# The down projection of one decoder layer as seven products of halves

## The chip, the core and the metric

One core of a Trainium2 chip runs the kernel once per call. Its engines work side by side: TensorE (PE: matmuls and their weight loads), VectorE (DVE), ScalarE (ACT), GpSimd (POOL), and SyncE (SP), which here only issues transfers. An engine does its instructions in the order of its program; waits between engines are semaphores. The metric is the device time of one call in microseconds (us), the lower the better.

## What is computed

One layer on 512 tokens of 1024 features, in fp32. Token mixing comes first and is not touched. The end of the layer is:

```
x  = x + merged @ w_out
up = conv(rms_norm(x) * ffn_norm @ w_up)        # 1024 -> 5632, causal, width 3
a  = silu(up[:2816]) * up[2816:]
x  = x + a @ w_down                              # 2816 -> 1024
out = x * rsqrt(mean(x * x) + 1e-6) * final_norm # over the 1024 features
```

## The kernel before

Every large fp32 product is done in three passes: each operand is split into a high part (a cast to the reduced format fp32r, on ACT) and a low part (the residue, a subtraction on DVE), and PE adds high x high, high x low and low x high (`split`, `wsplit`, `mm3`). Activations lie turned: features on the 128 partitions, the 512 tokens along the row, so that `hH[j]`, `hL[j]` are the parts of feature block j. Weights come through a pool `wp` with three buffers for each of three tags: `wr` (as loaded, 1024 columns, 512 KB, by `wtile` on SP's queue), `wh` and `wl` (the parts).

The up projection (`up`, `conv`) goes over 44 chunks of 128 features; each chunk is 24 matmuls of 128x512, then DVE, ACT, DVE, DVE scale and convolve it. Every second chunk gives one block of `a`, split into `aH[i]`, `aL[i]`, i = 0 to 21.

The down projection is done by feature: for output blocks j = 0 to 5 a bank `pd` sums 22 x 3 matmuls of 512 columns, weights as the stationary operand and `a` as the moving one. After each block DVE adds the residual `x1[j]`, ACT squares it, DVE sums the squares in `acc3`, ACT multiplies by the gain. For the last two blocks the weights `w_e` are loaded and split early (`eh`, `el`, in the memory that `hH`, `hL` leave); they are done for 384 tokens as above (`pA`, moving 384 columns) and for the last 128 tokens the other way round (`pB`, 256 columns), with tokens on the partitions. The norm of the 384 tokens is a mean over partitions (`rooted`, `over_partitions`) and is multiplied in while `pB` runs; that of the last 128 goes along the row, with six blocks turned by PE into `pTa`, `pTb`.

The order on each engine is set by a scheduler from the order and the dependences of the code: an instruction keeps to its engine's queue, and a tile of a pool waits until the tile that had its buffer is no longer read.

## Time and profile before

| | us |
|---|---|
| median of three runs (708.94 to 711.18) | 708.98 |
| the profiled execution | 709.26 |
| its span, from the first to the last instruction | 707.6 |
| PE busy in it | 699.6 |
| DVE busy | 476.5 |
| ACT busy | 331.5 |
| POOL busy | 12.3 |
| loads: 67 MB in all, mean over the span | 98 GB/s |

Times in the rows below count from the start of the span. The up projection's matmuls end at about 578.1, `pd` runs to 667.9, `pA` and `pB` to 701.2, and the output is written until 707.6. Busy time of PE is a sum of instructions that overlap one another (a 128x512 matmul is shown with 389 ns, while one starts each 0.23 us), so the pitch between starts is the measure, not the length shown.

### The profile page before, as it was taken

What the parts mean: (1) busy time and instruction counts of PE and PEld (TensorE: products, weight loads), DVE (VectorE), ACT (ScalarE), POOL (GpSimd) and SP (SyncE); (2) the same over time, 40 slices, a digit from 0 to 9 for tenths busy, and PEclk for the clock granted to TensorE, in tenths of its full rate; (3) what the DMA queues carried; (4) which work ended last, traced back from release to release, by engine and by line L of the source; (5) the groups of instructions that cost most, each with busy time, mean ns of one, the idle gap of its engine ahead of it and who ended that gap; (6) DMA issues with size and microseconds to landing.
All of it is one profiled execution on the core that took longest, in us unless ns stands there. A gap on an engine that the chain in (4) does not pass through costs nothing.

```text
span 707.6 us, 8629 instructions
## 1 busy us (share of the span) xinstructions
PE 699.6 (99%) x3303; PEld 586.6 (83%) x3303; DVE 476.5 (67%) x817; ACT 331.5 (47%) x496; POOL 12.3 (2%) x16
## 2 busy tenths in 40 slices
PE   9999999999999999999999999999999999999996
PEld 6888888888888888888888888888888888888896
DVE  8875799877777578755587777777677765433104
ACT  5464556676667533433454444444444444423101
POOL 0000110000000000000100000000000000000000
PEclk9999999999999999999999999999999999999999
DMA  8524422131121122523222233223322335631003
GB/s 260 179 77 135 168 83 82 60 113 40 69 72 60 33 87 76 190 94 105 93 98 89 90 102 107 90 90 100 108 89 91 95 98 163 194 87 48 0 1 120
DMA packets 22617, 69.63 MB, mean 98 GB/s; under 512 B 2736, under 2 KB 4400, under 8 KB 22576
## 3 DMA queue, kind: packets, MB, share of 16 engines
q1 hardware_dynamic: 21568, 66.72, 28.9%
q10 hardware_dynamic: 1008, 2.36, 0.9%
q8 instruction: 26, 0.43, 0.3%
q14 instruction: 15, 0.12, 0.1%
HBM read 66.97 MB, written 2.10 MB: 98 GB/s over the span
## 4 chain that ended last, share of the span: by engine, by line
PE 94%; DVE 3%; DMA 2%; issue 0%; ACT 0%; SPq 0%; POOLq 0%; DVEq 0%
PE pup L81 11%; PE pup L82 11%; PE pup L80 11%; PE pd L81 4%; PE pd L80 4%; PE pd L82 4%; PE pout L81 2%; PE pout L80 2%; PE pout L82 2%; PE pzb L82 2%; PE pzb L80 2%; PE pzb L81 2%; PE pv L80 2%; PE pv L82 2%; PE pza L81 2%; PE pv L81 2%
## 5 line engine op out<-in xcount | busy, mean ns | idle before, releaser
L70 ACT CAST wh_u<-wr_u 128x1024 fp32r<-128x1024 f32 x44 | 46.3, 1052 | 41.6 <-PE pup L81 29.5
L71 DVE TENSOR_TENSOR wl_u<-wr_u,wh_u 128x1024 fp32r<-128x1024 f32 x44 | 53.9, 1226 | 8.0 <-ACT wh_u L70 7.0
L604 DVE TENSOR_TENSOR z<-pup,r 128x512 f32<-128x512 f32 x44 | 30.2, 688 | 35.1 <-PE pup L82 35.1
L80 PE MATMUL pd<-aH,wh_d 128*128 128x512 f32 x132 | 51.3, 389 | 0.0
L81 PE MATMUL pd<-aL,wh_d 128*128 128x512 f32 x132 | 51.3, 389 | 0.0
L82 PE MATMUL pd<-aH,wl_d 128*128 128x512 f32 x132 | 51.3, 389 | 0.0
L70 ACT CAST wh_g<-wr_g 128x1024 fp32r<-128x1024 f32 x24 | 25.2, 1050 | 44.4 <-issue 23.3
L76 ACT CAST aH<-y 128x512 fp32r<-128x512 f32 x22 | 13.7, 621 | 56.7 <-DVE z L603 54.2
L71 DVE TENSOR_TENSOR wl_d<-wr_d,wh_d 128x896 fp32r<-128x896 f32 (+1 forms) x18 | 20.5, 1136 | 29.0 <-ACT wh_d L70 28.6
L70 ACT CAST wh_d<-wr_d 128x896 fp32r<-128x896 f32 (+1 forms) x18 | 17.7, 982 | 43.2 <-PE pd L81 35.2
L606 ACT ACTIVATE y<-z,part 128x512 f32<-128x512 f32 x44 | 35.9, 818 | 3.4 <-DVE z L604 1.8
L71 DVE TENSOR_TENSOR wl_g<-wr_g,wh_g 128x1024 fp32r<-128x1024 f32 x24 | 29.4, 1224 | 7.0 <-ACT wh_g L70 6.9
L610 DVE SCALAR_TENSOR_TENSOR y<-z,part,y 128x512 f32<-128x512 f32 x44 | 33.0, 752 | 1.4
L608 DVE SCALAR_TENSOR_TENSOR y<-z,part,y 128x512 f32<-128x512 f32 x44 | 32.8, 747 | 0.3 <-ACT y L606 0.3
L623 ACT ACTIVATE y<-y 128x512 f32<-128x512 f32 x22 | 13.9, 632 | 36.4 <-DVE y L610 36.4
L80 PEld LDWEIGHTS pd<-aH,wh_d 128*128 128x128 f32 x132 | 24.8, 188 | 5.2
L82 PEld LDWEIGHTS pd<-aH,wl_d 128*128 128x128 f32 x132 | 24.8, 188 | 5.2
L81 PEld LDWEIGHTS pd<-aL,wh_d 128*128 128x128 f32 x132 | 24.8, 188 | 5.1
L81 PE MATMUL pout<-mL,wh_o 128*128 128x512 f32 x64 | 25.4, 397 | 0.0
L82 PE MATMUL pout<-mH,wl_o 128*128 128x512 f32 x64 | 25.3, 395 | 0.0
L80 PE MATMUL pout<-mH,wh_o 128*128 128x512 f32 x64 | 25.2, 396 | 0.0
L77 DVE TENSOR_TENSOR aL<-y,aH 128x512 fp32r<-128x512 f32 x22 | 15.2, 693 | 14.2 <-ACT aH L76 14.2
(595 smaller groups left out, 2003.4 us busy)
## 6 DMA issues: line engine op xcount, KB each, us to landing
wr_u<-in_w_u_dram SPq DMA_DIRECT2D x44, 512.0 KB, 3.3
wr_g<-in_w_g_dram SPq DMA_DIRECT2D x24, 512.0 KB, 3.3
wr_d<-in_w_d_dram SPq DMA_DIRECT2D x12, 448.0 KB, 3.4
x<-in_xT_dram SPq DMA_DIRECT2D x16, 256.0 KB, 4.5
wr_v<-in_w_v_dram SPq DMA_DIRECT2D x8, 512.0 KB, 4.2
wr_o<-in_w_o_dram SPq DMA_DIRECT2D x8, 512.0 KB, 3.2
wr_d<-in_w_d_dram SPq DMA_DIRECT2D x6, 512.0 KB, 3.5
wr_e<-in_w_e_dram SPq DMA_DIRECT2D x5, 512.0 KB, 3.7
```

The lines of the kernel that those rows point to most:

```text
L70: A.copy(th[:, lo:hi], raw[:, lo:hi])
L71: V.tensor_tensor(out=tl[:, lo:hi], in0=raw[:, lo:hi], in1=th[:, lo:hi].bitcast(F32), op=ALU.subtract)
L76: A.copy(th, src)
L77: V.tensor_tensor(out=tl, in0=src, in1=th.bitcast(F32), op=ALU.subtract)
L80: T.matmul(o, lhsT=wh, rhs=xh, start=start, stop=False)
L81: T.matmul(o, lhsT=wh, rhs=xl, start=False, stop=False)
L82: T.matmul(o, lhsT=wl, rhs=xh, start=False, stop=stop)
L604: V.tensor_tensor(out=z[:, 2:], in0=pz, in1=r2, op=ALU.mult)
L606: A.activation(out=y, in_=z[:, 2:], func=AF.Identity, scale=part[:, w + 2:w + 3], bias=part[:, PCB + f:PCB + f + 1])
L608: V.scalar_tensor_tensor(out=y, in0=z[:, 1:S + 1], scalar=part[:, w + 1:w + 2], in1=y, op0=ALU.mult, op1=ALU.add)
L610: V.scalar_tensor_tensor(out=y, in0=z[:, 0:S], scalar=part[:, w:w + 1], in1=y, op0=ALU.mult, op1=ALU.add)
L623: A.activation(out=yg, in_=yg, func=AF.Silu)
```

## The change

The down projection becomes one product of two 2 x 2 matrices of halves: `a` by token halves (256 tokens) and by halves of its 2816 features (11 blocks), `w_down` by the same feature halves and by halves of the 1024 outputs. Eight products of halves become seven, after Winograd's form of Strassen's scheme:

- products of halves: P1 = A11 B11, P2 = A12 B21, P3 = S4 B22, P4 = A22 T4, P5 = S1 T1, P6 = S2 T2, P7 = S3 T3; in the code `product("1", ...)` to `product("7", ...)` in the order 1, 5, 2, 6, 3, 7, 4
- S1 = A21 + A22, S2 = S1 - A11, S3 = A11 - A21 on DVE, S4 = A12 - S2 on POOL; S2, S3 and S4 are written over A11, A21 and A12
- the differences of weights (`b11`, `b21`, `b22`, `t3_of`) are made on POOL, of weights as loaded, 1024 columns at a time (512 in the last step): T1 in product 1, T2 in product 2, T1 anew (B22 - B12) in product 3, and T4 = T2 - B21 in product 7
- the sums of products are added to the residual, partly on DVE from PSUM and partly on POOL (`plus`) after ACT or DVE has copied or added them.

Now tokens are on the partitions: `a` (high and low part, `ah`, `al`) is the stationary operand, the weights are the moving one, 512 columns wide. A product is 11 blocks x 2 token tiles x 3 passes = 66 matmuls of 128x512. Both its sides are split for it: the left half by `a_split` (three blocks, 1024, 1024 and 768 columns), the right half by `wsplit` in six steps. Product 4 does its two token tiles one after the other and splits its weights for each.

The residual `x1` is turned to tokens on partitions during the up projection (`x1_turn`, eight groups of four 128x128 transposes, copied back by ACT). `a` is kept unsplit in `aT`. The last norm is a sum along the row: `done` adds the product, squares with an accumulated sum on ACT, multiplies by the gain on DVE, and `finish` makes the root and scales and writes 128 tokens. `w_e` and the way through `pA`, `pB`, `pTa`, `pTb` are gone. B12, B21 and B22 are loaded twice, so 20.2 MB of weights come in the place of 11.5.

```diff
-    aH = [fp.tile([P, S], F32R, name=f"aH{i}") for i in range(NF)]
-    aL = [fp.tile([P, S], F32R, name=f"aL{i}") for i in range(NF)]
+    aT = fp.tile([P, NF, S], F32, name="aT")
...
+    def x1_turn(t, hf):
+        pt = bank(f"pt{t}{hf}")
+        for q in range(NT):
+            T.transpose(pt[:, q * P:(q + 1) * P], x1t[hf][:, q, t, :], ident)
+        A.copy(x1t[hf][:, :, t, :], pt.rearrange("p (q c) -> p q c", q=NT))
...
-        V.tensor_tensor(out=yv, in0=yg, in1=yv, op=ALU.mult)
-        split(aH[i], aL[i], yv)
+            V.tensor_tensor(out=aT[:, i], in0=yg, in1=yv, op=ALU.mult)
+            if 4 <= i < 12:
+                x1_turn((i - 4) // 2, i % 2)
...
+    def a_split(n, form):
+        parts = []
+        for lo, hi in blocks:
...
+            A.copy(h3, src)
+            V.tensor_tensor(out=al[:, :w].rearrange("p (k t) -> p k t", t=S2), in0=src, in1=h3.bitcast(F32),
+                            op=ALU.subtract)
+            parts.append((ah, al))
+        return parts
+    def product(n, form, weights):
+        banks = [bank(f"p{n}{m}") for m in range(2)]
+        parts = a_split(n, form)
+        for ms_ in ((0,), (1,)) if n == "4" else ((0, 1),):
+            for lo, hi in steps:
+                wh, wl = wsplit(weights(lo, hi), f"d{n}{lo}{ms_[0]}", 0, (hi - lo) * S)
+                for k in range(lo, hi):
...
+                    for m in ms_:
+                        ca = slice((k % 4) * S2 + m * P, (k % 4) * S2 + (m + 1) * P)
+                        mm3(banks[m], ah[:, ca], al[:, ca], wh[:, cw], wl[:, cw], k == 0, k == KH - 1)
+        return banks
...
+    def b11(lo, hi):
+        w = w_half(0, 0, "b11")(lo, hi)
+        w2 = w_half(0, 1, "b12")(lo, hi)
+        G.tensor_tensor(out=t1_of(lo, hi), in0=w2, in1=w, op=ALU.subtract)
+        return w
...
+    def t3_of(lo, hi):
+        w = w_half(1, 0, "b21b")(lo, hi)
+        G.tensor_tensor(out=t2_of(lo, hi), in0=t2_of(lo, hi), in1=w, op=ALU.subtract)
+        return t1_of(lo, hi)
...
+    s_ = product("1", A11, b11)
+    for m in range(2):
+        A.copy(p1[m], s_[m])
+        plus(m, 0, p1[m])
+    for lo, hi in blocks:
+        V.tensor_tensor(out=s1_of(lo, hi), in0=A21(lo, hi), in1=A22(lo, hi), op=ALU.add)
+    s_ = product("5", s1_of, t1_of)
...
+    s_ = product("2", A12, b21)
+    for m in range(2):
+        done(m, 0, s_[m])
...
+    for lo, hi in blocks:
+        G.tensor_tensor(out=A12(lo, hi), in0=A12(lo, hi), in1=A11(lo, hi), op=ALU.subtract)
+    s_ = product("3", A12, b22)
...
+    s_ = product("4", A22, t2_of)
+    for m in range(2):
+        with tc.high_priority():
+            done(2 + m, 0, s_[m], ALU.subtract)
+            finish(2 + m)
```

How the order moves on the engines. POOL, from its last instructions in the mixing part (`rv`) to its end, before: roots of a few numbers only.

```order
L531 TENSOR_TENSOR rv2_1490<-rv2_1490,mhalf_85 128x1
L531 TENSOR_TENSOR rv3_1735<-rv3_1735,mhalf_85 128x1
L148 TENSOR_TENSOR rt_f_3193<-ms_f_3192,mhalf_85 128x4
L148 TENSOR_TENSOR rt_A_5715<-ms_A_5714,mhalf_85 128x3
L730 TENSOR_TENSOR mB_5583<-mB_5583,mhalf_85 128x1
```

POOL from the same root `rt_f` on, after, to the third step of product 2 (`wr_db12...` and `wr_db11...` are loaded weights, `cp` and `ce` copies of products 1 and 5).

```order
L147 TENSOR_TENSOR rt_f_3128<-ms_f_3127,mhalf_84 128x4
L713 TENSOR_TENSOR t1_4885<-wr_db120_4915,wr_db110_4913 128x1024
...
L713 TENSOR_TENSOR t1_4885<-wr_db1210_5020,wr_db1110_5018 128x512
L719 TENSOR_TENSOR t2_0_4886<-wr_db220_5166,t1_4885 128x1024
L742 TENSOR_TENSOR x1_0_2765<-x1_0_2765,cp0_4895 128x4x128
L742 TENSOR_TENSOR x1_0_2765<-x1_0_2765,cp1_4896 128x4x128
L719 TENSOR_TENSOR t2_1_4887<-wr_db222_5187,t1_4885 128x1024
L786 TENSOR_TENSOR aT_3087<-aT_3087 128x4x256 x2
L742 TENSOR_TENSOR x1_1_2766<-x1_1_2766,ce0_4897 128x4x128 x2
L742 TENSOR_TENSOR x1_1_2766<-x1_1_2766,ce1_4898 128x4x128 x2
L786 TENSOR_TENSOR aT_3087<-aT_3087 128x3x256
L719 TENSOR_TENSOR t2_2_4888<-wr_db224_5208,t1_4885 128x1024
```

Between the root and the end of the kernel stand now 37 instructions on tensors: 24 differences of weights, 10 adds to the residual, 3 differences of the left half. The differences of product 2's third step stand behind four adds that need product 5.

SP, which issues the loads, where the up projection passes into the down projection, before (`wr_u43` is the last up chunk, `wr_d00` the first third of output block 0).

```order
L59 DMA wr_u42_4859<-in_w_u_dram 128x1024
L59 DMA wr_u43_4897<-in_w_u_dram 128x1024
L59 DMA wr_d00_4941<-in_w_d_dram 128x1024
L59 DMA wr_d08_4947<-in_w_d_dram 128x896
L59 DMA wr_d015_4953<-in_w_d_dram 128x896
L59 DMA wr_d10_5029<-in_w_d_dram 128x1024
```

After, to the second step of product 2 (`wr_db11` is B11, `wr_db12` B12, then `wr_db21` and `wr_db22`).

```order
L59 DMA wr_u42_4800<-in_w_u_dram 128x1024
L59 DMA wr_u43_4838<-in_w_u_dram 128x1024
L59 DMA wr_db110_4913<-in_w_d_dram 128x1024
L59 DMA wr_db120_4915<-in_w_d_dram 128x1024
L59 DMA wr_db112_4934<-in_w_d_dram 128x1024
L59 DMA wr_db122_4936<-in_w_d_dram 128x1024
...
L59 DMA wr_db1210_5020<-in_w_d_dram 128x512
L59 DMA wr_db210_5164<-in_w_d_dram 128x1024
L59 DMA wr_db220_5166<-in_w_d_dram 128x1024
L59 DMA wr_db212_5185<-in_w_d_dram 128x1024
```

Each step takes two buffers of three in the place of one, and the second is free again only when POOL has read it.

ACT at the same place, before (`y42`, `y21` and `y43` are the last chunks of the convolution, `wh_d` casts of weights, `aH` casts of `a`).

```order
L70 CAST wh_d00_4943<-wr_d00_4941 128x1024
L606 ACTIVATE y42_4850<-z42_4849,part_67 128x512
L76 CAST aH20_3132<-y42_4850 128x512
L70 CAST wh_d08_4949<-wr_d08_4947 128x896
L606 ACTIVATE y21_4891<-z21_4890,part_67 128x512
L623 ACTIVATE y21_4891<-y21_4891 128x512
L70 CAST wh_d015_4955<-wr_d015_4953 128x896
L606 ACTIVATE y43_4930<-z43_4929,part_67 128x512
L76 CAST aH21_3133<-y43_4930 128x512
L70 CAST wh_d10_5031<-wr_d10_5029 128x1024
```

After (`ah_10`, `ah_14`, `ah_18` are the casts of product 1's left half).

```order
L70 CAST wh_d100_4918<-wr_db110_4913 128x1024
L603 ACTIVATE y42_4793<-z42_4792,part_67 128x512
L70 CAST wh_d120_4939<-wr_db112_4934 128x1024
L603 ACTIVATE y21_4832<-z21_4831,part_67 128x512
L628 ACTIVATE y21_4832<-y21_4832 128x512
L70 CAST wh_d140_4960<-wr_db114_4955 128x1024
L603 ACTIVATE y43_4871<-z43_4870,part_67 128x512
L659 CAST ah_10_4901<-aT_3087 128x1024
L659 CAST ah_14_4905<-aT_3087 128x1024
L659 CAST ah_18_4909<-aT_3087 128x768
L70 CAST wh_d160_4981<-wr_db116_4976 128x1024
```

The casts of the first left half stand behind the last chunk's `y43`, while before the first output block could start with blocks of `a` that had been split long ago.

## Rows read from the trace of the kernel before

**Rows 1.** The page: busy time by engine, granted clock by slice, chain of waits.
```profile
PE 699.6 (99%) x3303; PEld 586.6 (83%) x3303; DVE 476.5 (67%) x817; ACT 331.5 (47%) x496; POOL 12.3 (2%) x16
...
PEclk9999999999999999999999999999999999999999
...
PE 94%; DVE 3%; DMA 2%; issue 0%; ACT 0%; SPq 0%; POOLq 0%; DVEq 0%
```

**Rows 2.** Windows at the end: start:end, length; busy us by engine; granted clock, DMA.
```profile
578.10:667.86 89.76, 89.76 (x397) 74.32 (x396) 34.51 (x44) 30.22 (x42) 0.00 (x0) 1.00 0.34 102
667.86:701.20 33.34, 33.31 (x219) 33.06 (x217) 8.09 (x18) 4.63 (x9) 0.86 (x1) 1.00 0.04 14
701.20:707.60 6.40, 0.00 (x0) 0.00 (x0) 1.87 (x6) 1.16 (x3) 0.55 (x1) 0.79 0.72 262
```

**Rows 3.** Tile view of pd: durations ns min/median/max, first and last start.
```profile
L80 PE MATMUL pd<-aH,wh_d x132: 389/389/389, 578.1 to 667.2; 128*128 128x512 f32 x132
```

**Rows 4.** Timeline of PE: start us, length us, engine, line, operation.
```profile
674.13 0.60 PE L693 MATMUL pTa<-cstt,x 128*128 128x128 f32 x4
674.56 0.38 PE L693 MATMUL pTb<-cstt,x 128*128 128x128 f32 x2
```

**Rows 5.** Timeline of DVE and ACT behind the last up-projection matmul.
```profile
578.30 0.69 DVE L604 TENSOR_TENSOR z<-pup,r 128x512 f32<-128x512 f32 x1 [2.11 <-PE pup L82]
...
581.67 0.69 DVE L625 TENSOR_TENSOR y<-y,y 128x512 f32<-128x512 f32 x1
...
582.40 0.62 ACT L76 CAST aH<-y 128x512 fp32r<-128x512 f32 x1 [2.49 <-DVE y L625]
```

**Rows 6.** Groups by line and shape: busy us, mean ns of one, idle before.
```profile
L71 DVE TENSOR_TENSOR wl_u<-wr_u,wh_u 128x1024 fp32r<-128x1024 f32 x44 | 53.9, 1226 | 8.0 <-ACT wh_u L70 7.0
...
L77 DVE TENSOR_TENSOR aL<-y,aH 128x512 fp32r<-128x512 f32 x22 | 15.2, 693 | 14.2 <-ACT aH L76 14.2
...
L71 DVE TENSOR_TENSOR wqL<-wr_q,wqH 128x768 fp32r<-128x768 f32 x4 | 3.8, 950 | 0.0
...
L70 ACT CAST wh_u<-wr_u 128x1024 fp32r<-128x1024 f32 x44 | 46.3, 1052 | 41.6 <-PE pup L81 29.5 <-PE pout L81 10.2 <-issue 1.9
```

**Rows 7.** Timeline of POOL, whole span.
```profile
70.63 1.10 POOL L515 TENSOR_SCALAR_AFFINE_SELECT wst<-wst 128x1024 f32<-128x1024 f32 x1 [32.35 <-DMA wst<-in_ws_t_dram]
...
104.45 0.92 POOL L531 TENSOR_TENSOR rv<-rv,mhalf 128x1 f32<-128x1 f32 x1 [8.89 <-DVE rv L530]
...
344.08 1.86 POOL L148 TENSOR_TENSOR rt_f<-ms_f,mhalf 128x4 f32<-128x4 f32 x1 [226.72 <-DVE ms_f L147]
694.88 0.86 POOL L148 TENSOR_TENSOR rt_A<-ms_A,mhalf 128x3 f32<-128x3 f32 x1 [348.94 <-DVE ms_A L147]
702.48 0.55 POOL L730 TENSOR_TENSOR mB<-mB,mhalf 128x1 f32<-128x1 f32 x1 [6.74 <-DMA out_dram<-x]
```

**Rows 8.** Timeline of DVE around POOL's instructions.
```profile
76.23 1.55 DVE L534 SCALAR_TENSOR_TENSOR vA<-vA,mv,gb 128x512 f32<-128x512 f32 x2
...
94.41 1.40 DVE L534 SCALAR_TENSOR_TENSOR vA<-vA,mv,gb 128x512 f32<-128x512 f32 x2
...
104.23 0.74 DVE L534 SCALAR_TENSOR_TENSOR vA<-vA,mv,gb 128x512 f32<-128x512 f32 x1
104.89 0.68 DVE L368 TENSOR_TENSOR za<-pza,rx 128x512 f32<-128x512 f32 x1
...
343.83 1.23 DVE L71 TENSOR_TENSOR wl_u<-wr_u,wh_u 128x1024 fp32r<-128x1024 f32 x1
```

**Rows 9.** DMA issues (KB each, us to landing); waits of SP's queue (total, times, longest).
```profile
wr_d<-in_w_d_dram SPq DMA_DIRECT2D x6, 512.0 KB, 3.5
...
SPq L59 <- DVE wl_d L71: 59.2, 15, 5.3
```

**Rows 10.** Timeline of the end: the last square and the output's issue.
```profile
701.21 0.38 ACT L726 ACTIVATE oB<-pB 128x256 f32<-128x256 f32 x1 [4.45 <-PE pB L82]
...
703.78 0.35 ACTq L734 DMA_DIRECT2D out_dram<-oB  x1
```

More of the change, by code (lines that the diff above doesn't have):

```diff
@@ new lines, in res, with b3, sums @@
+    def res(t, f):
+        return x1t[f][:, :, t, :]
+    def b3(t):
+        return t.rearrange("p (q c) -> p q c", q=NT)
+    def sums(i, t):
+        return fp.tile([P, S], F32, name=f"c{i}{t}")
+    ms = fp.tile([P, NT, 4], F32, name="ms")
+    gfb = fp.tile([P, D], F32, name="gfb")
+    A.dma_start(gfb, fnl.to_broadcast([P, D]))
+    A11, A12, A21, A22 = a_half(0, 0), a_half(0, 1), a_half(1, 0), a_half(1, 1)
+    t1 = fp.tile([P, KH * S], F32, tag="t1", name="t1")
+    t2 = [hp.tile([P, D], F32, tag=f"h{g}", name=f"t2_{g}") for g in range(6)]
@@ new lines, in block_kernel, with s1_of, t1_of, t2_of @@
+    s1 = [hp.tile([P, 4 * S2], F32, tag=f"h{6 + g}", name=f"s1_{g}") for g in range(2)]
+    s1.append(fp.tile([P, 3 * S2], F32, name="s1_2"))
+    def s1_of(lo, hi):
+        return s1[lo // 4][:, :(hi - lo) * S2].rearrange("p (k t) -> p k t", t=S2)
+    def t1_of(lo, hi):
+        return t1[:, lo * S:hi * S]
+    def t2_of(lo, hi):
+        return t2[lo // 2][:, :(hi - lo) * S]
+    def b11(lo, hi):
[3 more added lines that the diff above has]
+        return w
@@ new lines, in block_kernel @@
+    p1, p5 = ([sums(n, m) for m in range(2)] for n in "pe")
+    s_ = product("1", A11, b11)
[6 more added lines that the diff above has]
+    for m in range(2):
+        A.copy(p5[m], s_[m])
+        plus(m, 1, p5[m])
+        plus(2 + m, 1, p5[m])
+    s_ = product("2", A12, b21)
+    for m in range(2):
+        done(m, 0, s_[m])
@@ new lines, in block_kernel @@
+    for lo, hi in blocks:
+        V.tensor_tensor(out=A21(lo, hi), in0=A11(lo, hi), in1=A21(lo, hi), op=ALU.subtract)
+        V.tensor_tensor(out=A11(lo, hi), in0=s1_of(lo, hi), in1=A11(lo, hi), op=ALU.subtract)
+    s_ = product("6", A11, t2_of)
+    for m in range(2):
+        V.tensor_tensor(out=p1[m], in0=s_[m], in1=p1[m], op=ALU.add)
+        plus(m, 1, p1[m])
+    for lo, hi in blocks:
+        G.tensor_tensor(out=A12(lo, hi), in0=A12(lo, hi), in1=A11(lo, hi), op=ALU.subtract)
+    s_ = product("3", A12, b22)
@@ L738, in _layout @@
+    for m in range(2):
+        done(m, 1, s_[m])
+        finish(m)
+    s_ = product("7", A21, t3_of)
+    for m in range(2):
+        V.tensor_tensor(out=p1[m], in0=s_[m], in1=p1[m], op=ALU.add)
+        plus(2 + m, 0, p1[m])
+        done(2 + m, 1, p1[m])
+    s_ = product("4", A22, t2_of)
+    for m in range(2):
+        with tc.high_priority():
+            done(2 + m, 0, s_[m], ALU.subtract)
+            finish(2 + m)
 def _layout(x, positions, mix_norm, w_in, a_v_norm_g, a_v_norm_b, a_spatial_w, a_spatial_b, q_a_norm,
```

199 lines of the change are left out of this document (73 added, 126 removed).

## The prediction

> **What bounds the kernel now.** I read the page first: TensorE (PE) is busy for 699.6 of 707.6 us, the chain that ended last is PE for 94% of its length, and the granted clock is at its full level in every slice [rows 1]. Then the stretches of the end, since the change lies there: in 578.10 to 667.86 and 667.86 to 701.20 PE never pauses, while VectorE (DVE) works 34.5 of 89.8 us and 8.1 of 33.3 us, and GpSimd (POOL) almost nothing [rows 2]. So the down projection costs what PE takes, and what the others do is hidden. A stretch with 18 PE passes fewer gains if, and only if, the others keep up.
>
> The pitch of a 128x512 matmul comes from the tile view of pd: 132 triples, the first at 578.1, the last at 667.2, so 89.1 / 131 / 3 = 0.2267 us [rows 3]. The 389 ns in that row overlap each other and are not used.
>
> I call 578.1, where the up projection's last matmul has been issued, T0. The old end of PE is T0 + 123.1.
>
> **PE's part.** The old stage is 396 passes of 512 columns, 132 of 384 and 66 of 256: 528 in units of 512. Seven products of 11 blocks, 2 token tiles and 3 passes are 462, so 462 x 0.2267 = 104.7 us. The order shows that they are there, so the change does what its name says. The gain against 123.1 is 18.4 us, with 2.5 us of small matmuls and turns of the old stage that go too. Against it stand 32 turns of the residual in the up projection, where PE is the bound; four of the old stage's turns of the same shape start at 674.13 and the next group at 674.56 [rows 4], 0.11 each, so 3.5 us. A second loss is the start: ACT's casts of the first product's left half stand behind the last y of the conv, and take memory which the conv's tiles held. In the trace that chain runs from 578.30 to 582.36, and the next cast starts at 582.40 [rows 5]; it was hidden behind 21 of 22 blocks of the first pd. Now the first matmul waits for a 1.05 us cast [rows 6] behind it: T0 + 5.4. PE alone would therefore end at T0 + 3.5 + 5.4 + 104.7 = T0 + 113.6, 9.5 us earlier than now. That is the most that there is to win.
>
> **What the other engines get.** Weights are split into high and low parts once per use. Before, 22 x 1024 columns; now seven products of 5632 columns, and product 4 splits its weights twice, so 8 x 5632 = 44 x 1024. Left halves are split per product too, and the sums and differences are new. DVE's instructions after T0 with both inputs in SBUF, by the rows of [rows 6] (1.226 us for 1024 columns, 0.95 for 768, 0.69 for 512):
> - weight residues: 40 of 1024 and 8 of 512, two of the large ones ahead of T0: 38 x 1.226 + 8 x 0.69 = 52.1
> - residues of the left halves: 7 x (2 x 1.226 + 0.95) = 23.8
> - sums for S and A (s1, A21, A11), eight blocks: 9.0
> - end of the conv 2.2, gains and late adds 9 x 0.69 = 6.2.
>
> Together 93.3 us. With ten instructions that read one input from PSUM (6.9) and small ones, DVE has some 102 us in a stage of 105 us of PE: alone it would just fit. ACT's casts, 44 of 1024 columns for the weights and 7 x 2.75 for the left halves, are 63 x 1.05 = 66 us and have slack.
>
> POOL gets 24 differences of weights (20 of 1024 columns, 4 of 512), ten adds of 512, three differences of A12 (2816 columns in all) and four roots. No such instruction is in the trace. Its nearest row is the mask of 1024 columns with one input, 1.10 us [rows 7]. With two inputs the price lies between 1.10 (both read at once, as DVE does) and 2.20 (one after the other). Rows say which: the root at 104.45, alone 0.55 us at 702.48, took 0.92 and ended 0.40 after DVE's two-input instruction 104.23 to 104.97, though another DVE instruction, with one input in PSUM, ran over its end [rows 7, 8]. So POOL reads by the path over which DVE reads its second SBUF input. One path reads two inputs in two passes: I take 2.2 us for 1024 columns. Keeping 1.1 for a rival, POOL has after T0 (three of the large differences come before it) 17 x 2.2 + 4 x 1.1 + 10 x 1.1 + 6.05 + 3 x 0.55 = 60.5 us.
>
> **The path that they share.** The same is seen at the other places. rt_f (four columns) starts at 344.08 and ends at 345.94, 0.88 after DVE's weight residue (343.83 + 1.23 = 345.06) had ended; rt_A, with three columns and DVE idle, takes 0.86 [rows 7, 8]. POOL did nothing while DVE read two SBUF inputs. Whether DVE also waits for POOL shows weakly: a pair of DVE instructions with the root between them took 1.55 us at 76.23 and 1.40 at 94.41 [rows 8]. It is not needed for the sum: if POOL can't read in DVE's 93.3 us, its 60.5 us come on top.
>
> The Trainium skill, page "SBUF — State Buffer", section "Who interferes with whom", speaks against this change in the same way: a DVE instruction with two SBUF inputs and a GpSimd one that reads SBUF exclude each other, whichever starts second being blocked for the whole of the first. The rows above agree for POOL as the second; no row here has POOL long enough to show DVE as the second. If DVE gave no way at all, the sum would stay as it is; by the rule DVE's splits also stall behind each difference, and PE behind them.
>
> The page "GPSIMD Engine Reference", section 3.1, gives 4497 ns for a two-input fp32 add of 2048 columns; half of that, an estimate of 2.25 us for 1024, would make the sum 1.4 us longer.
>
> Sum: 93.3 + 60.5 = 153.8 us of exclusive work, against 105 of PE. To it comes time in which both wait. The right operands of a difference arrive in pairs through three buffers, and SP issues the next load only when POOL (or the split) has freed one; a load lands 3.5 us after issue [rows 9]. Before, the same queue waited for DVE 15 times with 59.2 us in all [rows 9] and it cost nothing, as PE had its weights. For product 1 I take three pairs as loaded ahead of T0, one in each of the last chunks of 24 x 0.2267 = 5.4 us. In products 2 and 3 each second difference or so waits for a load with only 1.9 us of DVE work beside it (one residue and a share of the left half's): 6 x 1.6 = 9 us. It could be nothing (other splits fill it) or 25 us (POOL's queue also stands behind the four adds that wait for product 5, with three differences and their loads behind them).
>
> **The end.** Before, from PE's end at 701.2 to the end of the span 6.4 us [rows 2]: a square of 256 columns (0.38), small steps, a root and a product until the issue of the output at 703.78 [rows 10], then the transfer. Now a subtraction of 0.69 stands ahead of the square, the square has 512 columns (estimate: 0.25 more), and there is one small step more (estimate: 0.2); root, product and a transfer of 256 KB stay: 1.1 us more, 7.5.
>
> Forecast: 578.1 + 3.5 + 153.8 + 9 + 1.0 (last matmuls behind the last residue) = 745.4; + 7.5 = 752.9 of span. The profiled execution lasts 709.26 for a span of 707.6, 1.7 more, and lies 0.3 above the median of the three: **755 us**.
>
> **Rivals.**
> 1. *As forecast, the shared path sets the end*: 735 (no idle time, loads fill) to 775.
> 2. *PE's clock falls too.* PE now works 105 of 165 us with a pause in nearly every step; the trace of before has no pause of this kind ahead of 701.2, and the mean granted clock in the stretch after it is 0.79 [rows 2]. At the lower level (1.2 GHz) all seven products take 462 x 0.453 = 209 us, which would be the bound: 806. With half of them, 780. For it: five microseconds without a matmul right at T0. Against it: a step is 12 x 0.2267 = 2.7 us of PE against 1.2 + 0.6 + 2.2 = 4.1 us of the shared path, so most pauses are of 1.4 us.
>
>  The page "TensorE: Matmul & The Clock Gate", Part 1, says that idle gaps between bursts return PE to half its clock; no run here shows that yet.
> 3. *POOL reads two inputs at once*: 1.1 us for 1024 columns, POOL 31 us instead of 60.5, so 725 (712 to 735). For it: one input took 1.10. Against: the shared path.
> 4. *The other side: no exclusion at length.* The roots are tiny; a long difference may interleave with DVE. Then PE is the bound: 578.1 + 3.5 + 5.4 + 104.7 + 7.5 + 1.7 = 701, with 0 to 8 us of load waits: 701 to 709, middle 705. It decides from the point at which POOL's work outside DVE's is under 699.8 - 578.1 - 3.5 - 10 - 93.3 = 15 of its 60.5 us, which is 0.54 us for 1024 columns. For it: nothing but the shortness of the rows. Against: rt_f waited for 0.98 us of a single instruction.
>
> **How the numbers follow.** Rival 1 has 0.57, rival 2 0.15, rival 3 0.13, rival 4 0.15 (0.11 below 707, 0.03 within 2 us of now, 0.01 above). Within 0.3% is about what a measurement of this kernel can tell from no change. Faster 0.11, same 0.03, slower 0.86. The range reaches from 716 (most of rival 3, weight 0.12) over all of rival 1 to 795 (0.12 of rival 2): 0.81.
>
> **What would show it.** POOL differences of about 2.2 us where DVE is idle, and longer ones, or long DVE residues, where both run; DVE plus POOL near 150 us in the stage with PE at 60 to 70%; the waits of PE in products 2, 3, 7 and 4 ended by DVE's residues or POOL's differences. I am wrong if a difference of 1024 columns and DVE residues run over each other at 1.2 us each, if PE's row stays at 9s (rival 4), or if the granted clock drops for many us (rival 2). The start is right if the first matmul of product 1 comes 5 to 6 us after the last of the up projection, the turns if the up projection ends 3 to 4 us later.

## The result, and the profile after

The changed kernel takes 767.22 us (median of four runs, 766.05 to 770.75), the kernel before 708.96 in the same comparison. The ratio is 1.082 (95% interval 1.078 to 1.087): slower by 8%, and 12 us above the 755 that was forecast. The profiled execution took 767.71 us for a span of 766.0. Other runs below are single executions, each beside one of the kernel before (709.1 to 710.0); the four runs of the changed kernel spread over 0.6%, so differences of 2 to 3 us between single runs are read from places in the traces.

The page of the changed kernel: busy time, the span in 40 slices (19.2 us each; a digit is the busy share in tenths), and the chain that ended last.

```profile
PE 713.0 (93%) x3183; PEld 581.3 (76%) x3183; DVE 564.5 (74%) x841; ACT 356.8 (47%) x521; POOL 112.6 (15%) x55
...
PE   9999999999999999999999999999995896697675
...
DVE  8775999777686886557676666767679786866985
...
POOL 0100000000000000000000000000014569444721
PEclk9999999999999999999999999999998889698878
...
PE 77%; POOL 6%; DVE 6%; DMA 5%; issue 3%; ACT 1%; SPq 0%; POOLq 0%; ACTq 0%; DVEq 0%
```

Up to slice 30 PE stands at 9 as in [rows 1]. From slice 31 on, the down projection, PE has gaps, POOL works as never before, and the granted clock, full in every slice of [rows 1], falls under 9 tenths in many.

Windows of the changed kernel, one for the pause after the up projection, one for each product in the order 1, 5, 2, 6, 3, 7, 4, and the tail (start:end, length, busy us of each engine with its number of instructions, then granted clock, DMA share, GB/s):

```profile
581.40:590.87 9.47, 0.12 (x1) 0.03 (x1) 9.47 (x10) 3.17 (x5) 4.24 (x2) 0.76 0.31 112
590.87:613.84 22.97, 20.01 (x66) 14.73 (x67) 17.70 (x14) 8.19 (x10) 13.47 (x3) 0.80 0.21 70
613.84:631.21 17.37, 16.94 (x67) 13.07 (x67) 14.68 (x10) 9.57 (x12) 13.06 (x5) 0.91 0.45 149
631.21:662.25 31.04, 20.93 (x68) 15.29 (x67) 21.41 (x12) 9.06 (x12) 24.11 (x10) 0.78 0.41 122
662.25:682.21 19.96, 16.99 (x67) 13.33 (x66) 14.52 (x14) 9.72 (x14) 4.98 (x2) 0.91 0.30 101
682.21:705.22 23.01, 17.77 (x68) 12.95 (x66) 14.90 (x12) 8.46 (x10) 12.25 (x6) 0.94 0.47 151
705.22:733.22 28.00, 21.05 (x67) 15.68 (x66) 25.16 (x19) 10.99 (x16) 18.43 (x9) 0.81 0.44 130
733.22:757.87 24.65, 19.06 (x67) 13.69 (x65) 19.99 (x23) 12.70 (x18) 5.59 (x3) 0.86 0.08 22
757.87:766.00 8.13, 0.17 (x1) 0.00 (x0) 2.15 (x5) 1.44 (x3) 0.55 (x1) 0.65 0.24 65
```

A product has 66 matmuls and would take 15.4 us without a stop. None does: they take 17 to 31 us, the stage 176.5 us (581.4 to 757.87) in the place of 123.1 [rows 2]. PE is idle for 43.6 us of it (176.47 - 132.85). What its matmuls waited for (us in total, times, longest):

```profile
PE p L81 <- DVE wl_d L71: 20.3, 14, 4.8
PE p L80 <- ACT wh_d L70: 13.7, 4, 7.8
PE p L80 <- ACT ah L659: 9.4, 1, 9.4
```

The first are low parts of weights, made by DVE. The second are four high parts, and in all four ACT's cast had itself waited for a load. The third is the pause ahead of product 1. A pause is here, and in what follows, PE's idle time as the profile shows it; the expectations below count from start to start, which gives 0.17 us more. PE's busy time is 132.8 us for matmuls that need 107.8 at full clock; most of the rest is matmuls behind pauses that run at a lower clock. DVE is busy for 137.8 us and POOL for 96.1, waits for each other included; one of them at least is busy for 156.7 of the 176.5 us (the union of their timelines).

**POOL and DVE keep each other out, in both directions.** Timelines of the changed kernel at three places (start, length, engine, line, operation):

```profile
565.79 2.40 POOL L713 TENSOR_TENSOR t<-wr_db,wr_db 128x1024 f32<-128x1024 f32 x1 [220.50 <-DMA wr_db<-in_w_d_dram]
...
573.99 2.52 POOL L713 TENSOR_TENSOR t<-wr_db,wr_db 128x1024 f32<-128x1024 f32 x1 [5.80 <-DMA wr_db<-in_w_d_dram]
...
574.28 2.77 DVE L607 SCALAR_TENSOR_TENSOR y<-z,part,y 128x512 f32<-128x512 f32 x1
...
589.53 9.74 POOL L713 TENSOR_TENSOR t<-wr_db,wr_db 128x1024 f32<-128x1024 f32 x1 [5.22 <-DMA wr_db<-in_w_d_dram]
...
594.66 2.35 DVE L780 TENSOR_TENSOR aT<-s,aT 128x1024 f32<-128x1024 f32 x2
597.69 2.67 DVE L71 TENSOR_TENSOR wl_d<-wr_db,wh_d 128x1024 fp32r<-128x1024 f32 x1 [0.68 <-ACT wh_d L70]
```

An undisturbed difference of 1024 columns takes 2.40 us. The second runs from 573.99 to 576.51; DVE's step of the convolution, issued at 574.28, ends at 577.05, which is 0.54 behind that, and has taken 2.77 us instead of 0.75: DVE waited for POOL. At 589.53 POOL waits for DVE: DVE has instructions with two SBUF inputs in an unbroken row until 597.01, POOL's difference ends 2.26 later, and the residue that DVE starts at 597.69 ends 1.09 after that again.

### The profile page after: what moved, and what is told of

Read it like the earlier page. It is cut to its first block, busy times and chain, and to the rows that moved or that the text cites. A ratio compares the mean times of both kernels' runs of the same rounds, so it can differ in the third digit from the quotient of the medians.

```text
span 766.0 us, 8535 instructions
## 1 busy us (share of the span) xinstructions
PE 713.0 (93%) x3183; PEld 581.3 (76%) x3183; DVE 564.5 (74%) x841; ACT 356.8 (47%) x521; POOL 112.6 (15%) x55
## 4 chain that ended last, share of the span: by engine, by line
PE 77%; POOL 6%; DVE 6%; DMA 5%; issue 3%; ACT 1%; SPq 0%; POOLq 0%; ACTq 0%; DVEq 0%
PE pup L80 10%; PE pup L81 10%; PE pup L82 10%; DMA wr_db<-in_w_d_dram 3%; DVE wl_d L71 2%; POOL t L713 2%; PE pout L81 2%; PE pout L80 2%; PE pout L82 2%; PE pv L80 2%; PE pzb L80 2%; PE pzb L82 2%; PE pzu L82 2%; PE pzu L80 2%; PE pzu L81 2%
## 5 line engine op out<-in xcount | busy, mean ns | idle before, releaser
L81 PE MATMUL p<-wl_d,ah 128*128 128x512 f32 x154 | 71.0, 461 | 20.5 <-DVE wl_d L71 20.3
L80 PE MATMUL p<-wh_d,ah 128*128 128x512 f32 x154 | 68.2, 445 | 23.1 <-ACT wh_d L70 13.7
L82 PE MATMUL p<-wh_d,al 128*128 128x512 f32 x154 | 67.9, 442 | 0.0
L81 PEld LDWEIGHTS p<-wl_d,ah 128*128 128x128 f32 x154 | 33.3, 217 | 36.1 <-DVE wl_d L71 28.7
L80 PEld LDWEIGHTS p<-wh_d,ah 128*128 128x128 f32 x154 | 33.6, 218 | 33.7 <-ACT wh_d L70 15.5
L713 POOL TENSOR_TENSOR t<-wr_db,wr_db 128x1024 f32<-128x1024 f32 (+1 forms) x6 | 22.6, 3771 | 244.9 <-DMA wr_db<-in_w_d_dram 244.9
L71 DVE TENSOR_TENSOR wl_d<-t,wh_d 128x1024 fp32r<-128x1024 f32 (+1 forms) x30 | 41.3, 1391 | 5.0 <-ACT wh_d L70 5.0
L82 PEld LDWEIGHTS p<-wh_d,al 128*128 128x128 f32 x154 | 33.7, 219 | 7.9 <-DVE al L660 0.6
L70 ACT CAST wh_d<-t 128x1024 fp32r<-128x1024 f32 (+1 forms) x30 | 28.8, 972 | 20.1 <-PE p L82 10.5
L71 DVE TENSOR_TENSOR wl_g<-wr_g,wh_g 128x1024 fp32r<-128x1024 f32 x24 | 29.4, 1223 | 7.0 <-ACT wh_g L70 6.9
L660 DVE TENSOR_TENSOR al<-aT,ah 128x1024 fp32r<-128x1024 f32 (+1 forms) x18 | 28.6, 1596 | 6.5 <-ACT ah L659 6.5
L71 DVE TENSOR_TENSOR wl_d<-wr_db,wh_d 128x1024 fp32r<-128x1024 f32 (+1 forms) x12 | 21.4, 1789 | 15.4 <-ACT wh_d L70 15.4
L659 ACT CAST ah<-aT 128x1024 fp32r<-128x1024 f32 (+1 forms) x18 | 17.4, 975 | 25.0 <-PE p L81 18.7
```

Source lines behind the costliest of these rows:

```text
L70: A.copy(th[:, lo:hi], raw[:, lo:hi])
L71: V.tensor_tensor(out=tl[:, lo:hi], in0=raw[:, lo:hi], in1=th[:, lo:hi].bitcast(F32), op=ALU.subtract)
L80: T.matmul(o, lhsT=wh, rhs=xh, start=start, stop=False)
L81: T.matmul(o, lhsT=wh, rhs=xl, start=False, stop=False)
L82: T.matmul(o, lhsT=wl, rhs=xh, start=False, stop=stop)
L659: A.copy(h3, src)
```

## The experiments

The sum in the prediction rests on three statements: POOL's reads and DVE's two-input instructions exclude each other, their sum is the bound, and the rest (start, loads, clock) is small. The rivals after the result: POOL is only slow; the loads through three buffers are late; the layout by token costs, not the scheme.

**Short differences.** The 24 weight differences on 8 of their columns.

```diff
+    G.memset(t1, 0.01)
+    for t_ in t2:
+        G.memset(t_, 0.01)
...
-        G.tensor_tensor(out=t1_of(lo, hi), in0=w2, in1=w, op=ALU.subtract)
+        G.tensor_tensor(out=t1_of(lo, hi)[:, :8], in0=w2[:, :8], in1=w[:, :8], op=ALU.subtract)
```

> The 24 differences of weights on POOL work on the first 8 columns of each step only; the rest of T1, T2 and T4 is filled once with a constant, so those products are not the layer's. Loads, buffers, waits, splits and matmuls stay. Theory (POOL's reads and DVE's two-input instructions exclude each other, so their sum sets the stage): POOL loses some 55 of 70 us of work, DVE's 102 us and PE's 105 us remain, the seven products take 105 to 115 us in place of 167, total 708 to 720. Rival 'ring' (the pairs of loads through three buffers set the pace, each waiting for POOL's release and then 3.8 us): the releases and loads stay, so at least 745. Rival 'clock' (PE at its lower level sets the length): follows the pauses, no forecast of its own, the granted clock would go back to 1.00 here.

Measured: 737.77 us, 29.5 less. The reads of the differences are half of the loss, but the number that the theory gave was missed: some 29 us stay above the kernel before, so something else costs as much. The rival of the loads gave at least 745 and missed too; the granted clock, mean of the stage, comes to 0.91 and not to 1.00. The time in which DVE or POOL works falls from 156.7 to 115.9 us, by 41 as their sum demands, the stage only from 176.5 to 146.5: both stand idle for 30 us of it, so in this run their sum alone is no longer the bound.

**Busy, but reading nothing.** Short differences, and in the code behind each of them two POOL memsets.

```diff
+        G.tensor_tensor(out=t1_of(lo, hi)[:, :8], in0=w2[:, :8], in1=w[:, :8], op=ALU.subtract)
+        for _ in range(2):
+            G.memset(t1_of(lo, hi)[:, 8:], 0.01)
```

> As the kernel with short differences, but POOL also fills the rest of each step's T twice with a constant (two memsets of 1016 columns, some 2.1 us together by the 0.52 us of a 512-column one), so POOL is busy about as long as with the differences but reads nothing; the products with T are not the layer's. Theory (it is POOL's reading that excludes DVE's second SBUF input): as with the short differences, 708 to 722. Rival 'slow POOL' (POOL's own 2.4 us for each step, on the way from the load to the buffer's release and to T, sets the pace without any exclusion): as the changed kernel, 750 to 770. Rival 'ring': at least 745.

Measured: 737.7 us, the same as with short differences. Windows from the up projection's end to PE's end, the changed kernel first, then short differences, then with memsets:

```profile
581.40:757.87 176.47, 132.85 (x463) 98.78 (x462) 137.83 (x107) 71.87 (x90) 96.12 (x38) 0.85 0.34 106
```
```profile
581.40:727.90 146.50, 120.30 (x465) 92.39 (x463) 110.07 (x107) 71.88 (x89) 51.92 (x40) 0.91 0.38 125
```
```profile
581.40:727.90 146.50, 119.72 (x465) 91.38 (x463) 109.13 (x107) 71.98 (x89) 78.46 (x77) 0.91 0.38 125
```

POOL is busy for 78.5 us instead of 51.9, and PE and DVE don't notice. DVE has the same 107 instructions in all three, and 28 us less in the second and third. How POOL's writes and DVE's two-input instructions pass each other, at one place:

```profile
656.75 7.21 POOL L742 MEMSET t<- 128x1016 f32 x9
...
658.01 1.23 DVE L660 TENSOR_TENSOR al<-aT,ah 128x1024 fp32r<-128x1024 f32 x1 [1.27 <-ACT ah L659]
659.15 1.22 DVE L71 TENSOR_TENSOR wl_d<-t,wh_d 128x1024 fp32r<-128x1024 f32 x1
```

In this run nine residues of 1024 columns have only memsets beside them and take 1.22 us in the mean; in the changed kernel, from 575 us on, 24 such residues with no POOL instruction beside them take 1.22, and 29 with one that reads beside them take 1.98, the longest 3.43. So it is POOL's reading that slows DVE, not its being busy. The run is weaker against "POOL is only slow" than it was meant to be: in the order of the trace only 8 of the 24 short differences have a memset right behind them, 12 of the 48 memsets ran at 347 us, and none stands among the differences from 636.87 to 647.29 in product 2, where loads wait for POOL. How much of the 29.5 us is POOL's own time on the way to a buffer's release, and not exclusion, is not separated by it. The Trainium skill says of the exclusion, page "SBUF — State Buffer", section "Who interferes with whom": a DVE instruction with two SBUF inputs contends with a GpSimd instruction that reads SBUF, not with one that only writes it; the residues agree. The same page of the Trainium skill says that issue order decides who blocks; the difference at 589.53 above was issued ahead of the two sums at 594.66 and still waited behind them, so who comes first among waiting ones isn't told by the order of issue alone.

**Differences on DVE.** The same 24 instructions, whole, on DVE.

```diff
-        G.tensor_tensor(out=t1_of(lo, hi), in0=w2, in1=w, op=ALU.subtract)
+        V.tensor_tensor(out=t1_of(lo, hi), in0=w2, in1=w, op=ALU.subtract)
```

> The 24 differences of weights move from POOL to DVE (1.23 us each for 1024 columns in place of 2.4), nothing else. Theory: work on the shared path falls from 93 + 62 to 93 + 27 + 15 us (POOL keeps its adds and A12); DVE is then the bound with some 102 + 27 = 129 us: products 130 to 142 us in place of 167, total 730 to 745. Rival 'ring': the next load still waits for the difference and then for 3.8 us, 755 to 767. A rival by which POOL and DVE don't disturb each other would see DVE go from 102 to 129 us of work and win nothing: 765 or more.

Measured: 740.63 us, in the theory's range. The stage in this run:

```profile
581.40:730.40 149.00, 119.93 (x464) 89.95 (x463) 134.57 (x128) 72.41 (x90) 35.07 (x16) 0.92 0.39 122
```

DVE is busy for 134.6 us of 149.0, POOL for 35.1, one of them at least for 135.6. One engine with all the weight work is 27 us faster than two that share it: a difference of 1024 columns takes DVE 1.2 us where POOL takes 2.4 and holds DVE up.

**A fourth weight buffer.** The second weight of a difference in a buffer of its own, so that it needn't wait in the row of three.

```diff
+            t = dp.tile([P, 2 * S], F32, tag="w2", name=f"w2_{n}{lo}", bufs=1)
+            SY.dma_start(t[:, :(hi - lo) * S], w_d[k, f, :, lo * S:hi * S])
```

> The second weight of each pair gets a buffer of its own (a fourth one beside the three of the ring), so that the right operand's loads run further ahead; work on all engines stays. Theory: the sum on the shared path stays, only time in which both wait falls: 752 to 767. Rival 'ring': the pace of the loads was the bound, 715 to 740.

Measured: 770.39 us, no gain, and above both ranges. But the edit does not do what it was meant to. All the second weights of products 1, 2 and 3 now share one buffer (`bufs=1`), so a second weight is loaded only when POOL has read the one before it. POOL in product 1:

```profile
602.49 2.35 POOL L720 TENSOR_TENSOR t<-w_b,wr_db 128x1024 f32<-128x1024 f32 x1 [3.85 <-DMA w_b<-in_w_d_dram]
608.41 2.37 POOL L720 TENSOR_TENSOR t<-w_b,wr_db 128x1024 f32<-128x1024 f32 x1 [3.57 <-DMA w_b<-in_w_d_dram]
614.64 2.35 POOL L720 TENSOR_TENSOR t<-w_b,wr_db 128x1024 f32<-128x1024 f32 x1 [3.86 <-DMA w_b<-in_w_d_dram]
```

Each of these waits a whole load, and the first difference starts at 591.78 in the place of 565.79, since the buffer's memory is free late. So no run shows what a deeper row of buffers would give. That the loads are not the bound by themselves is told by the runs with short differences and with differences on DVE: they leave the row of three as it is and fall under what this rival gave (737.8 against at least 745, 740.6 against 755 to 767). Their share is open: the four pauses of the changed kernel that end with a cast behind a load sum to 13.7 us.

**POOL's other reads short too.** Short differences, and also its ten adds and the three differences of A12 on 8 columns.

```diff
-        G.tensor_tensor(out=res(t, f), in0=res(t, f), in1=b3(t_), op=ALU.add)
+        c = (slice(None), slice(0, 1), slice(0, 8))
+        G.tensor_tensor(out=res(t, f)[c], in0=res(t, f)[c], in1=b3(t_)[c], op=ALU.add)
-        G.tensor_tensor(out=A12(lo, hi), in0=A12(lo, hi), in1=A11(lo, hi), op=ALU.subtract)
+        G.tensor_tensor(out=A12(lo, hi)[c], in0=A12(lo, hi)[c], in1=A11(lo, hi)[c], op=ALU.subtract)
```

> All of GpSimd's work on two SBUF inputs in the down projection is cut to 8 columns: the weight differences, the ten adds of 512 and the three differences of A12 (the rest of them is left out). With short differences alone 737.7 us were measured, with pauses of 7.0 us in product 2, 3.0 in product 3 and 4.9 in product 4. Theory A (GpSimd's remaining reads hold VectorE, and its adds stand ahead of the next differences): the pauses in products 2 and 4 fall under 2 us each and the time to 715 to 726 us. Theory B (what is left is the load after a buffer is freed, and VectorE's own order): the pauses stay, 733 to 738 us.

Measured: 720.67 us, 17.1 less again, in theory A's range. Product 2 takes 15.9 us instead of 26.8, its longest pause 0.2 instead of 6.8; the pause in product 4 goes from 4.8 to 2.6, above the 2 that was given. How the same instructions of DVE (residues of the left halves, 1024 columns) shrink, grouped by shape in the changed kernel, with short differences, and with all of POOL's reads short (count, busy us, mean ns of one):

```profile
L660 DVE TENSOR_TENSOR al<-aT,ah 128x1024 fp32r<-128x1024 f32 x12 | 21.2, 1773 | 6.5 <-ACT ah L659 6.5
```
```profile
L660 DVE TENSOR_TENSOR al<-aT,ah 128x1024 fp32r<-128x1024 f32 x12 | 15.7, 1315 | 5.3 <-ACT ah L659 5.2
```
```profile
L660 DVE TENSOR_TENSOR al<-aT,ah 128x1024 fp32r<-128x1024 f32 x12 | 14.6, 1223 | 7.3 <-ACT ah L659 7.3
```

1223 ns is the undisturbed price of [rows 6]. This is the clearest form of the result: nothing about these twelve instructions changed but what POOL read meanwhile.

Product 2 shows how a POOL instruction holds the whole line. Timelines of the changed kernel:

```profile
635.51 8.71 POOL L742 TENSOR_TENSOR x<-x,ce 128x512 f32<-128x512 f32 x4
644.18 2.81 POOL L786 TENSOR_TENSOR aT<-aT 128x768 f32<-128x768 f32 x1
646.95 4.63 POOL L719 TENSOR_TENSOR t<-wr_db,t 128x1024 f32<-128x1024 f32 x2
...
653.20 1.04 ACT L70 CAST wh_d<-wr_db 128x1024 fp32r<-128x1024 f32 x1 [10.97 <-DMA wr_db<-in_w_d_dram]
...
654.30 0.80 PE L80 MATMUL p<-wh_d,ah 128*128 128x512 f32 x1 [7.78 <-ACT wh_d L70]
```

The four late adds of product 5 and the last of A12 stand in POOL's queue ahead of T2's differences; the weights that these read keep their buffers until 649.28 and 651.58, so the next load is issued late, the cast on ACT waits 10.97 us for it, and PE 7.78.

**Own memory for product 1's left half.** Its high and low parts go to memory that T2 takes later, so that they needn't wait for the tiles of the convolution.

```diff
+            if n == "1":
+                ah, al = own[lo // 4], own[3 + lo // 4]
```

> The high and low parts of product 1's left half get memory of their own (that which T2 takes later), so that their split need not wait for the last tiles of the convolution; nothing is left out. Theory (the pause of 9.4 us ahead of product 1 is the wait for these tiles and for what VectorE does ahead of the residue): the pause falls to 2 to 5 us, and the half-clock matmuls behind it shrink; 757 to 763 us against 767 us. Rival (VectorE's and GpSimd's shared work is the bound throughout, so an early start only meets the next wait): the pause shrinks, and the time is 765 to 768 us.

Measured: 764.8 us (span 763.1 against 766.0), between the two. The start did what it should: last matmul of the up projection and first of product 1, in the changed kernel and in this run:

```profile
581.13 0.39 PE L82 MATMUL pup<-h7f,wl_u 128*128 128x512 f32 x1
590.87 0.77 PE L80 MATMUL p<-wh_d,ah 128*128 128x512 f32 x1 [9.36 <-ACT ah L659]
```
```profile
581.43 0.39 PE L82 MATMUL pup<-h7f,wl_u 128*128 128x512 f32 x1
581.66 0.39 PE L80 MATMUL p<-wh_d,own 128*128 128x512 f32 x1
```

The first matmul comes 9.2 us earlier, PE's last one only 2.9 earlier (754.76 against 757.64 start to start). Product 5 alone takes 6.6 us longer. The mechanism is the rival's: time won at one place is lost at the next, since DVE and POOL hold the pace.

**Product 4 splits once.**

```diff
-        for ms_ in ((0,), (1,)) if n == "4" else ((0, 1),):
+        for ms_ in ((0, 1),):
```

> Product 4 splits its weights once for both token tiles, not once for each; nothing is left out. It takes 5.5 x 1.226 = 6.7 us from VectorE in the last product, after GpSimd's differences are done. Theory (the last product, too, waits for splits, and its single pause of 4.9 us lies at VectorE's late adds): product 4 gets some 3 us shorter and that pause stays, 762 to 766 us. Rival (the pause is the second splitting itself): the pause goes too, 757 to 761 us. Against both: the two tiles end together and the last steps double, up to 2 us.

Measured: 760.22 us, 7.0 less: the rival's range. Product 4 takes 18.7 us from its first matmul to its last instead of 24.4, its longest pause is 1.7 us instead of 4.8; the tail grows from 8.1 to 10.0 us. So VectorE's late adds did not hold it alone. A likely reason, not shown by itself: with 12 matmuls to a step in the place of 6, PE has twice the work under which a split is hidden.

**All of it at once.** POOL's reads short, own memory for product 1, product 4 split once.

> All causes named so far are taken away at once: GpSimd's two-input work is on 8 columns only (the rest of it is left out), product 1's left half has its own memory, product 4 splits its weights once for both token tiles. If they are all that there is, TensorE is nearly the bound: 581 + 3 to 5 for the start + 462 x 0.2332 = 107.7 + 8 for the end + 1.7 = 702 to 704, with 3 to 8 us of single pauses 705 to 712 us. If a cause is missing, 718 to 730 us.

Measured: 709.82 us, no different from the kernel before (709.94 on the same chip). Windows from the first matmul of the products to PE's end, with POOL's reads short alone, and with everything:

```profile
581.40:710.90 129.50, 114.66 (x463) 87.98 (x462) 97.02 (x107) 71.69 (x89) 28.97 (x40) 0.96 0.44 140
```
```profile
582.85:698.01 115.16, 109.39 (x463) 85.99 (x461) 87.68 (x96) 62.55 (x78) 29.55 (x42) 1.00 0.47 153
```

So 57 of the 58 us between the two kernels go in three steps: 29.5 with the reads of the differences, 17.1 with POOL's other reads, 10.9 with the start and the double split of product 4. PE is busy for 109.4 of 115.2 us and the granted clock is full. And with all sums of the scheme almost free, the scheme is still no faster than the kernel before: its stage is 7.9 us shorter than the 123.1 of [rows 2], but the up projection ends 4.8 us later than there, and the end behind PE takes 3.7 more (10.1 against 6.4).

**The layout without the scheme.** Eight plain products of halves by token; no sums, no differences, and no second splitting in any product.

```diff
+    for t in range(2):
+        for f in range(2):
+            banks = [bank(f"p{t}{f}{m}") for m in range(2)]
+            for k in range(2):
+                product(f"{t}{f}{k}", a_half(t, k), w_half(k, f, f"{t}{f}{k}"), banks, k == 0, k == 1)
```

> The down projection by token as eight plain products of halves: weights are split at each use, the residual and the last norm are as in the changed kernel, but no sum, no difference and no late add. TensorE has 528 passes: 581 + 9 (start) + 528 x 0.2332 = 123.1 + 8 + 1.7 = 723; VectorE 8 x (5.5 x 1.226 + 3.4) = 81 us has no partner that shares its path. Theory (it is the differences and what hangs on them that cost, not the layout by token): 718 to 728 us, TensorE without pauses over 1 us behind the start. Rival (splits of left halves and loads cost as much by token alone): 735 to 750 us.

Measured: 725.09 us, in the theory's range. One product more and 42 us faster than the scheme. The layout by token costs 15 us against the kernel before: the up projection ends 3.6 us later (turns), the first matmul comes 5.8 us behind it, the products take 126.1 us in the place of 123.1 (the longer pitch, and the lower clock at the start of the first), and the end takes 3.4 more. Within the products PE has no pause over 0.2 us, so splitting per product costs nothing there. The other 42 us are the scheme's, one product less included: its sums and differences, and product 4's second splitting, which was 7.0 by itself.

**Where the pitch comes from.** The matmuls of the products came every 0.2333 us, those of the old stage every 0.2267. The run with own memory had 0.2267 in product 1, behind pauses too, and 0.2333 in all others. What differs is where the left half lies. In the program's memory map the weights, within 512 bytes, start at 224 and the left halves at 288; in the stretches at 0.2267 both operands start at 224. Two runs of the plain products with an unused tile ahead of the left halves, of 64 bytes per partition and of 448 (112 in the place of 16 in the line shown):

```diff
+    fp.tile([P, 16], F32, name="shift")
     dp = ctx.enter_context(tc.tile_pool(name="dp", bufs=2))
```

> The eight plain products by token, with one unused tile of 64 bytes per partition ahead of the pool of the left halves, so that both operands of a matmul start at the same place within 128 bytes (before: 96 for the weights, 32 for the left halves). In the traces matmuls whose operands agree there come every 0.2267 us (up projection, old down projection, product 1 where its left half lies elsewhere), those that differ every 0.2332 us (the products, the output projection). Theory (place): the pitch falls to 0.2267, 528 x 0.0066 = 3.5 us less, 721 to 722.5 us against 725.1. Rival (the role of the operands, or a pause ahead): the pitch stays and the time is 724.5 to 725.7 us.

> As the run with 64 bytes, but with an unused tile of 448 bytes per partition: then both operands start at the same place within 512 bytes (224), as they do in every stretch of the traces that runs at 0.2267 us. With 64 bytes the places were 224 and 352, and the pitch went from 0.2333 to 0.2324. Theory (place within 512 bytes): 0.2267, 721 to 722 us. Rival (something else about the memory of product 1's left half): 0.232 to 0.233, 723.5 to 725.5 us.

Measured: 723.85 and 721.60 us. Tile view of the products (durations min/median/max in ns, first and last start), without the shift, with 64 bytes, with 448:

```profile
L82 PE MATMUL p<-wh_d,al x176: 390/398/793, 588.6 to 713.3; 128*128 128x512 f32 x176
```
```profile
L82 PE MATMUL p<-wh_d,al x176: 390/393/796, 588.4 to 712.1; 128*128 128x512 f32 x176
```
```profile
L82 PE MATMUL p<-wh_d,al x176: 388/389/792, 588.4 to 709.8; 128*128 128x512 f32 x176
```

The last stretch is 3.3 us shorter than the first, and the pitch between neighbours is 0.2333, 0.2324 and 0.2267 us. The first guess, the place within 128 bytes, fell with the run of 64 bytes; with the same place within 512 the pitch is the full 0.2267. Whether it is the sameness or the left half's own place is not separated: in all these stretches the weights start at 224, and in short stretches of the mixing part where both operands start at 256 (`pq`) the mean intervals are 0.227 to 0.233 us.

**What the runs point to, together.** Differences on DVE, own memory, product 4 split once, left halves shifted by 64 bytes.

> The changed kernel with all that the runs point to and nothing left out: differences of weights on VectorE, own memory for product 1's left half, product 4's weights split once, the left halves shifted by 64 bytes. With the differences on VectorE it and GpSimd worked 137 of 150 us after the up projection; 7 us less of splits leaves 130, so theory (VectorE with what excludes it is the bound): 581 + 130 + 5 to 12 of waits + 8 + 1.7 = 726 to 733 us. Rival (single waits were the bound, as in the run with all of them taken away): 712 to 720 us. Faster than the kernel before, under 707 us, by neither.

Measured: 736.78 us, above both ranges, only 3.9 less than with the differences on DVE alone. DVE works 127.2 of 142.7 us of the stage. The early start makes a new wait: product 5's first low part of weights stands in DVE's queue behind the rest of product 1's differences and the sums for S1, and PE waits 7.1 us for it until 605.99. The work of DVE and POOL is near the 130 us that were given (128.1); the waits were too low, 14.7 us in which neither works against 5 to 12, and the end takes 10.0 us against 8.

## Why the prediction was right

767 us lies in the range of 716 to 795, in the likeliest case's own 735 to 775, and the sign is right. That the shared path sets the length is borne out by runs in which nothing is left out. The time in which DVE or POOL works, and the stage's length, are 156.7 of 176.5 us in the changed kernel, 156.9 of 173.5 with the early start, 148.2 of 167.4 with product 4 split once, 135.6 of 149.0 with the differences on DVE and 128.1 of 142.8 with all of that together: the stage follows the sum at a distance of 13 to 20 us. Step by step:

- **The shared path**: as forecast. Price of a POOL difference of 1024 columns: 2.2 forecast, 2.33 to 2.41 measured where DVE was not in its way. The reason that was given, one path that reads two inputs in two passes, agrees with the price, but no run isolates it. DVE's own work: 102 us forecast, 97.0 in the run where POOL reads next to nothing. The exclusive sum: 153.8 forecast, 156.7 measured as the union of both. The question that the rows of before left open, whether DVE waits for POOL too, is answered by the 2.77 us at 574.28: it does. The Trainium skill's rule on the page "SBUF — State Buffer", section "Who interferes with whom", holds in this trace for both directions. The estimate of 2.25 us from the page "GPSIMD Engine Reference" of the Trainium skill, section 3.1, is a little below the 2.33 to 2.41 measured.
- **Idle time of both**: this term was mis-sized. 9 us were forecast (0 to 25), and 1 for the last matmuls; 19.7 were measured (176.5 - 156.7), eight gaps over 0.8 us among them with 15.5 in all. That and the 2.9 us of the union are the 12.5 us by which PE's end came later than 745.4. (6 x 1.6 is 9.6, not 9; it changes nothing.) Five of the eight gaps, 10.1 us, end when a load lands: these were foreseen in kind (POOL's queue behind the four adds) and put in the range, not in the middle. The other three, 5.4 us, end when PE lets go of a buffer that ACT's next cast needs; this the forecast did not have.
- **The clock**: rival 2 half came true, on top of the first and not in its place. The reason against it, pauses of 1.4 us, failed: there are pauses of 7.78, 4.77 and 3.50 us. The row of the 7.78 us pause stands above; windows before it, in it, behind it:

```profile
640.00:646.50 6.50, 6.40 (x27) 4.54 (x25) 4.81 (x3) 2.00 (x2) 6.50 (x3) 1.00 0.28 83
646.50:654.30 7.80, 0.02 (x2) 0.00 (x1) 0.02 (x1) 1.10 (x2) 5.08 (x3) 0.80 0.50 167
654.30:660.40 6.10, 5.63 (x12) 4.08 (x13) 6.10 (x3) 2.38 (x3) 4.79 (x2) 0.50 0.40 112
```

 At 0.50, the 1.2 GHz level, 12 matmuls behind the pause take 6.1 us; 27 ahead of it took 6.5. Of the stage's 176.5 us, 9.4 are the first pause, 34.2 the others and 107.8 matmuls at the full clock. Of the 25.1 that are left most are matmuls at the lower one: 114 intervals between starts are 0.26 to 0.63 us long, 21.9 us more in all than at the full pitch. How much of that reached the end was not separated, since no run kept the pauses and not the clock. The page "TensorE: Matmul & The Clock Gate" of the Trainium skill, Part 1, which says that gaps bring PE back to half its clock, is borne out by these rows.
- **Turns**: 3.5 us forecast; the up projection ends at 581.36 (its last matmul starts at 581.13 and takes a pitch) instead of 578.1, 3.3 later.
- **The start**: 5.4 us forecast, 9.4 measured. The step counted the conv's last chain and one cast. It missed that DVE's order puts sums for S1 and A21 and a weight residue ahead of the conv's last steps, and that this residue waits for POOL (2.77 us at 582.63). But the whole pause is worth 2.9 us only, since the shared path sets the pace behind it.
- **PE's part**: 104.7 us forecast, 107.8 at the pitch that the layout gives (462 x 0.2333). The pitch of pd was taken over for operands that lie elsewhere; pout in the kernel before, at 0.2335, would have told. The passes saved are 66 (528 to 462); the 18 in the prediction's first paragraph are the 18.4 us.
- **The tail**: 7.5 forecast, 8.1 measured; outside the span 1.7 as forecast.
- **Rivals 3 and 4** fall: a difference of 1024 columns takes 2.33 us and more and not 1.1, and the exclusion holds at length.

The misses on the start and on PE's pitch cost the forecast little, since PE was not the bound; that is the case's doing, not the forecast's. What the forecast did not see although it came out right is how little is won by taking one cause away. Short differences were expected at 708 to 720 us and gave 737.8: their sum fell as forecast, but waits of both engines, which the forecast holds at 9 us, grew to 30. POOL's ten adds and three A12 differences, 17 us in POOL's own sum, cost 17.1 us of time there; they also stand ahead of what loads wait for.

## What to carry to other kernels

Fewer matmuls help only if the sums that buy them have an engine that is free, and free means free of shared paths: here a product saved is 15.4 us of PE, and the kernel with seven is 42 us slower than the one with eight plain ones (7 of them for product 4's second splitting). Work that has two inputs in SBUF is best counted for DVE and POOL together, as one resource; moved from POOL to DVE it was 27 us cheaper here. The sum of both is where to start, and the waits come on top: they were 13 to 20 us where the sum was the bound, and 30 where it no longer was. And where PE leaves the bound, its pauses bring matmuls at the lower clock (12 in 6.1 us behind the longest one), a cost that no run here has priced by itself.
